# Output copy of the attention on VectorE, the last group's product behind the second tile's power, and the MLP's first low parts on VectorE alone

## The chip, the cores and the metric

The kernel runs on one core of a Trainium2 chip. The metric is the device time of one execution in microseconds. The engines are called by the profile's names: PE (TensorE, matmuls, with PEld for its weight loads), DVE (VectorE), ACT (ScalarE), POOL (GpSimd) and SP (SyncE, which here issues most DMAs). Each engine works through its own queue in order; semaphores tie the queues together.

## The reference

One layer for two groups of tokens, 256 context tokens and 2048 latent tokens, of width 1024. For each group, in float32:

```
h = RMSNorm(x) * (1 + scale1) + shift1
q, k, v, f = split(h @ w_in)                      # 4 heads x 2 halves x 64; v 4 x 128; f 4 x 128
a = softmax(q1 k1) - lam * softmax(q2 k2)         # differential attention, latent rows see 512 cached + 2048 keys
attn = RMSNorm(a @ v) * subln_g * (1 - lam_init)  # per head
four = real(fft2(f)) @ w_four
x += gate1 * (concat(attn, four) @ w_out)
h = RMSNorm(x) * (1 + scale2) + shift2
x += gate2 * (relu(h @ w1) ** 2 @ w2)             # 1024 -> 4096 -> 1024
```

The outputs are both groups' x and the context tokens' keys and values.

## The kernel before

**Products.** A float32 product is made of three fast products: each operand is split into a high part (a cast) and a low part (the value minus the high part), and `mm3` issues high x high (L95), high x low (L96) and low x high (L97). So ahead of every product there is a cast, mostly on ACT, and a subtraction, mostly on DVE.

**Stages.** Projection, Fourier mixing, attention (about 550 to 1244 us), output projection with the second norm (to 1460 us), the MLP's first product, the MLP's second product. Inside a stage the order of each engine's queue is the order in which the program calls its pieces (`tc.manual_schedule`).

**Attention.** Four heads, each in groups of 256 queries; a class `Group` holds a group's pieces as methods. A table of events (time, method) is filled for all groups and sorted by time, and that is the order in which the pieces are called; the time has no other meaning. Per group: scores on PE (`Ss`, L1081), row maxima on DVE (L1086), exps on ACT (`P0s`, `P1s`, L1105), the combination of the two softmaxes on POOL (L1120, L1121), transposes on PE (`pts`, L1136), high parts on ACT (`ahs`) and low parts on DVE (`als`, L1148), and the product with v into `po`. A group's end is `o1` to `o9`: `o1` copies the sum out of `po` to `oTs` (L1173), `o2` transposes it on PE (L1177), `o3` copies that to `os` (L1184), `o4` squares it on ACT (L1190), `o5` takes the power -1/2 on POOL, `o6` and `o7` send the result through memory and back as `rbs`, spread over all partitions, `o8` multiplies `oTs` by `rbs` on POOL (L1211), `o9` stores it as `att`. For the very last group everything from `o4` on is put in a list, LASTO, and called later, between pieces of the output projection.

**Output projection.** 18 tiles of 128 tokens, in the order `seq`. The first three are s0, s1, s2. `mix(i)` makes a tile's high part `mh` (L1603) and low part `ml` (L1605) on DVE; `w_split` splits w_out into `woh` (ACT, L1576) and `wol` (DVE, L1577 and L1580); `out_mm` issues the products, `out_post` applies the gate (L1623, L1624), `x_norm` makes the second norm. In the norm ACT sums squares (`nsqb`, L229), DVE scales (`nssb`, L230), POOL takes the power -1/2 (`nrsb`, L92), DVE multiplies (`xn`, L236); PE then transposes `xn` (`ptb`, L249).

**First product of the MLP.** A seven-product scheme (of Strassen's kind) over quarter matrices: ORDER = (1, 6, 2, 7, 5, 4, 3), one item of 12 PE products for each in a round, `pA` to `pD` being their sums. `h_parts` makes the high part `mhh` (ACT, L1502) and the low part `mhl` (DVE, L1506) of an activation operand of 128x1536; for the third to fifth operand the low part is split in two halves, POOL's and DVE's (L1511). `w_cast` makes a weight operand's `ophW` (ACT, L1468) and `oplW` (DVE, L1474). `mlp_ahead` loads, prepares and casts the first operands while the output projection still runs.

Of the kernel before, what the change touches and what calls it, by code (L numbers as in the profile page):

```python
# [21 lines left out]
KD = D // P  # L22
NP = 256
NS = 2048
NT = NP + NS
PAST = 512
H = 4
# [10 lines left out]
def f32(ap):  # L38
    return ap.bitcast(F32)


def body(tc, a, out):
    nc = tc.nc
    ctx = ExitStack()
    with ctx:
# [211 lines left out]
        right = ExitStack()  # L257
# [732 lines left out]
        with ExitStack() as c3_:  # L990
# [49 lines left out]
            class Group:  # L1040
# [130 lines left out]
                def o1(self):  # L1171
                    self.oT = self.op.tile([P, 256], F32, tag="oT", name=f"oT{self.nm}", bufs=1 if self.last else 3)
                    nc.scalar.copy(self.oT, self.po[:, 0:256])  # L1173

# [134 lines left out]
            for h in range(H):  # L1309
# [19 lines left out]
                for g in range(hd.ng):  # L1329
# [31 lines left out]
                    w = base + (AVS + 5) * T + 1.0 * u  # L1361
                    for t, fn in ((0, gr.o1), (0.4, gr.o2), (0.75 if gr.last else 4.25, gr.o3), (8.5, gr.o4), (9.2, gr.o5), (11.8, gr.o6), (16.3, gr.o7), (23.4, gr.o8), (26.0, gr.o9)):
                        if gr.last and t > 1:
                            LASTO.append(fn)
                        else:
                            add(w + t * u, fn)
# [122 lines left out]
        def h_parts(b, p):  # L1489
# [17 lines left out]

            def rest2():
                t = src[0][1]
                for V, c in ((nc.gpsimd, slice(2, 4)), (nc.vector, slice(0, 2))):  # L1510
                    V.tensor_sub(lo[:, c, :], t[:, c, :], f32(hi[:, c, :]))  # L1511

            if b == 0 and p in ORDER[2:5]:
                return high, rest2

            return high, rest
# [11 lines left out]
        def mlp_ahead(part):  # L1528

            if part == 0:  # L1530
                h_prep(0, ORDER[0])
            elif part == 3:
                for n in range(2):
                    if n:
                        h_prep(0, ORDER[n])
                    w_cast(n)
                    w_low()
                    if n == 0:
                        h_load(0, ORDER[3])
            elif part == 1:  # L1540
                h_load(0, ORDER[4])
                w_cast(2)
                w_cast(3)
            else:
                R = RAW[0]
                nc.vector.tensor_sub(R["a12"], R["a12"], R["s2"])
                R["s4"] = R["a12"]
# [6 lines left out]
        with c3o, ExitStack() as c4, ExitStack() as c4x, ExitStack() as c4w:  # L1554
# [44 lines left out]
            def mix(i):  # L1599
# [3 lines left out]
                nc.vector.tensor_copy(mh, mT)  # L1603
                for c in (slice(0, 2), slice(2, KD)) if i == s0 else (slice(0, KD),):
                    nc.vector.tensor_sub(ml[:, c, :], mT[:, c, :], f32(mh)[:, c, :])  # L1605
# [52 lines left out]
            with tc.manual_schedule():  # L1658
# [29 lines left out]
                x_norm(s0)  # L1688
                for fn in LASTO[3:]:
                    fn()  # L1690
                kv_even.close()
                ms1 = ctx.enter_context(tc.tile_pool(name="m_s1", bufs=2, side="right"))
                ms2s = ctx.enter_context(tc.tile_pool(name="m_s2s", bufs=2, side="right", reuse_waits="tile"))
                mix_load(seq[3])
# [3 lines left out]
                x_store(s1)  # L1698
                x_norm(s1)
                for n, i in enumerate(seq[2:], 2):  # L1700
                    if n == 2:
# [38 lines left out]
        with c5r, ExitStack() as c5:  # L1740
# [157 lines left out]
            with tc.manual_schedule():  # L1898
                for n, (q, p) in enumerate(ITEMS):
# [3 lines left out]
                    rest = None  # L1903
                    if n == 3:
                        mlp_ahead(2)
                        w_add(1, 0)
                    if n < 4:
# [6 lines left out]
                    if n == 5:  # L1914
                        high, rest = h_parts(0, 3)
                        high()
                    w_low()
                    for c in CASTS[n] if n < len(CASTS) else (n + LEAD + 1,):
# [247 lines left out]
```

## Time and profile before

| | |
|---|---|
| median of 3 runs (lowest to highest) | 2858.12 us (2855.85 to 2858.37) |
| profiled execution | 2859.23 us |
| its span | 2857.4 us |
| granted TensorE clock, mean | 0.996 |
| PE busy | 2826.0 us, 99% of the span |
| DVE busy | 1991.7 us, 70% |
| ACT busy | 1538.3 us, 54% |
| POOL busy | 1083.1 us, 38% |

The shares are means over stages that differ: in attention DVE, ACT and POOL are all busy most of the time, in the MLP's second product POOL hardly is. Rows of a timeline give start, duration, engine, line, operation, output <- input, and in brackets the idle time before and what ended it. Rows of the windows view give the stretch, its length, the busy time of PE, PEld, DVE, ACT and POOL with the number of instructions, the granted clock, the DMA share and GB/s. Records of matmuls overlap: the next one starts before the last one's end as shown.

### The profile page before, as it was taken

The page shows a single profiled execution, that of the slowest core. Times are in us where ns is not written, and L with a number is a line of the kernel's source. Part 1 is how long each engine was busy: PE and PEld are TensorE (multiplying, and loading weights), DVE is VectorE, ACT ScalarE, POOL GpSimd, SP SyncE. Part 2 cuts the span into 40 slices and gives each one's busy share as a digit, 9 for nine tenths or more (in the row PEclk, how much of TensorE's full clock was granted, in tenths as well). Part 3 has the DMA queues.
Part 4 walks back from the last instruction along what each step waited for, and adds up shares of the span by engine and source line. Part 5 has one row for each costly group of instructions (what it writes and reads, how often), then busy time and mean ns, then how long its engine had stood idle before and what let it go on. Part 6 is the DMA issues. An engine that isn't in the chain of part 4 may idle for free.

```text
span 2857.4 us, 43074 instructions
## 1 busy us (share of the span) xinstructions
PE 2826.0 (99%) x15029; PEld 2455.7 (86%) x15029; DVE 1991.7 (70%) x3357; ACT 1538.3 (54%) x3479; POOL 1083.1 (38%) x893
## 2 busy tenths in 40 slices
PE   8999999999999999999999999999999999999999
PEld 5888888688888888888889999999998888888887
DVE  7767887888888888864477777778775353445554
ACT  4333323798999989843356565566554332233221
POOL 1211223689999899942223333333332000000000
PEclk9999999999999999999999999999999999999999
DMA  7777767432222333156867667667647464445663
GB/s 285 220 209 200 232 208 240 163 108 55 80 75 53 112 63 85 40 137 207 251 209 232 224 240 234 218 224 239 227 167 256 147 202 138 136 144 186 206 205 111
DMA packets 404491, 497.69 MB, mean 174 GB/s; under 512 B 31427, under 2 KB 320304, under 8 KB 401202
## 3 DMA queue, kind: packets, MB, share of 16 engines
q1 hardware_dynamic: 398656, 484.09, 53.7%
q0 software_dynamic: 2064, 7.67, 0.8%
q10 hardware_dynamic: 3554, 3.17, 0.4%
q8 instruction: 119, 1.95, 0.3%
q14 instruction: 98, 0.80, 0.1%
HBM read 317.30 MB, written 179.62 MB: 174 GB/s over the span
## 4 chain that ended last, share of the span: by engine, by line
PE 54%; DMA 1%; DVE 0%; issue 0%; SPq 0%; POOL 0%; ACT 0%; DVEq 0%; POOLq 0%
PE ps L95 8%; PE ps L97 8%; PE ps L96 8%; PE pB L1782 2%; PE pB L1783 2%; PE pB L1781 2%; PE pC L1781 2%; PE pC L1782 2%; PE pC L1783 2%; PE pA L1781 2%; PE pA L1783 2%; PE pA L1782 2%; PE po L97 2%; PE po L95 2%; PE po L96 2%; PE pD L1783 1%
## 5 line engine op out<-in xcount | busy, mean ns | idle before, releaser
L1086 DVE TENSOR_REDUCE mxs<-Ss 128x1 f32<-128x512 f32 x636 | 405.8, 686 | 83.6 <-PE Ss L1081 73.3
L1443 DVE TENSOR_TENSOR sl<-sr,sh 128x768 fp32r<-128x768 f32 x168 | 161.8, 964 | 331.5 <-ACT sh L1442 331.1
L1121 POOL TENSOR_TENSOR P0s<-P0s,P1s 128x1024 f32<-128x1024 f32 (+2 forms) x128 | 377.2, 2946 | 10.7
L1442 ACT CAST sh<-sr 128x768 fp32r<-128x768 f32 x168 | 140.6, 838 | 418.3 <-PE ps L96 418.3
L1823 POOL TENSOR_TENSOR gs<-g,g 128x384 f32<-128x384 f32 x48 | 69.7, 1453 | 454.4 <-ACT g L1793 435.9
L1105 ACT ACTIVATE P1s<-Ss,mxs 128x512 f32<-128x512 f32 x318 | 215.4, 694 | 35.9 <-DVE mxs L1089 33.8
L95 PE MATMUL pj<-wh,hh 128*128 128x512 f32 x576 | 228.7, 397 | 2.0 <-DVE hh L556 2.0
L95 PE MATMUL ps<-thT,sh 128*128 128x512 f32 x585 | 227.6, 389 | 0.0
L96 PE MATMUL ps<-tlT,sh 128*128 128x512 f32 x585 | 227.6, 389 | 0.0
L97 PE MATMUL ps<-thT,sl 128*128 128x512 f32 x585 | 227.6, 389 | 0.0
L96 PE MATMUL pj<-wl,hh 128*128 128x512 f32 x576 | 227.0, 394 | 0.0
L97 PE MATMUL pj<-wh,hl 128*128 128x512 f32 x576 | 225.8, 392 | 0.0
L1105 ACT ACTIVATE P0s<-Ss,mxs 128x512 f32<-128x512 f32 x318 | 214.6, 692 | 4.9 <-DVE mxs L1089 4.0
L1136 PE MATMUL pts<-ident,P0s 128*128 128x128 f32 x1280 | 192.4, 274 | 4.5 <-DVE als L1148 1.8
L1081 PE MATMUL Ss<-KS0s,Qs 128*128 128x512 f32 x636 | 190.8, 421 | 0.4 <-ACT P1s L1105 0.4
L1081 PE MATMUL Ss<-KS1s,Qs 128*128 128x512 f32 x636 | 189.2, 422 | 1.5 <-ACT P0s L1105 1.1
L1792 ACT ACTIVATE g<-uz 128x384 f32<-128x384 f32 x144 | 75.7, 526 | 200.2 <-DVE uz L1815 170.6
L1136 PEld LDWEIGHTS pts<-ident,P0s 128*128 128x128 f32 x1280 | 152.3, 141 | 36.1 <-issue 5.2
L1120 POOL TENSOR_SCALAR P1s<-P1s,tots 128x1024 f32<-128x1024 f32 (+2 forms) x128 | 171.7, 1341 | 5.8
L1148 DVE TENSOR_TENSOR als<-pts,ahs 128x512 fp32r<-128x512 f32 x256 | 163.7, 681 | 8.6 <-ACT ahs L1143 8.6
L95 PE MATMUL ps<-ophT,sh 128*128 128x512 f32 x423 | 164.7, 389 | 1.1 <-DVE uz L1815 1.1
L96 PE MATMUL ps<-oplT,sh 128*128 128x512 f32 x423 | 164.6, 389 | 0.0
(539 smaller groups left out, 8030.8 us busy)
## 6 DMA issues: line engine op xcount, KB each, us to landing
sr<-sd SPq DMA_DIRECT2D x84, 768.0 KB, 4.5
a<-in_w SPq DMA_DIRECT2D x184, 256.0 KB, 4.2
sd<-gs SPq DMA_DIRECT2D x192, 192.0 KB, 1.9
sd<-g SPq DMA_DIRECT2D x144, 192.0 KB, 2.4
wm<-in_w_mod SPq DMA_DIRECT2D x32, 512.0 KB, 5.0
Qs<-qd SPq DMA_DIRECT2D x32, 512.0 KB, 5.4
b<-in_w SPq DMA_DIRECT2D x64, 256.0 KB, 5.5
b<-tsum SPq DMA_DIRECT2D x64, 256.0 KB, 4.6
```

What stands on the lines that cost most here:

```text
L95: nc.tensor.matmul(ps, lh, rh, start=first, stop=False)
L96: nc.tensor.matmul(ps, lh, rl, start=False, stop=False)
L97: nc.tensor.matmul(ps, ll, rh, start=False, stop=last)
L1081: nc.tensor.matmul(S[:, :w], self.Q[:, x, m, j * P:j * P + P], self.hd.KS[m][:, b * 512:b * 512 + w], start=(x == 0), stop=(x == 1))
L1086: nc.vector.tensor_reduce(self.mx[j][:, m, b:b + 1], self.S[j, m, b], axis=AX.X, op=ALU.max)
L1105: nc.scalar.activation(dst, S, AF.Exp, bias=self.mx[j][:, m, 6:7], accum_out=self.sm[j][:, m, b:b + 1])
L1120: nc.gpsimd.tensor_scalar(p, p, tot[:, 3:4], 0.0, op0=ALU.mult, op1=ALU.add)
L1121: nc.gpsimd.tensor_add(d, d, p)
L1136: nc.tensor.transpose(pt[:, c:c + P], self.p0[j][:, (kb + t) * P:(kb + t + 1) * P], ident)
L1781: nc.tensor.matmul(ps, wh[:, c], hh[:, k, :], start=first and k == 0, stop=False, skip_group_check=True)
L1782: nc.tensor.matmul(ps, wh[:, c], hl[:, k, :], start=False, stop=False, skip_group_check=True)
L1783: nc.tensor.matmul(ps, wl[:, c], hh[:, k, :], start=False, stop=k == 3, skip_group_check=True)
```

## The change

Five edits:

1. `o1` copies `po` to `oTs` on DVE, where it was on ACT (32 copies of 128x256).
2. `o3` of one group, the third from last of the last head, stands at 2.5 in the event table, where it was at 4.25.
3. `mix` splits the low part `ml` in 256 + 768 columns for the first two tiles; it did for the first.
4. The last group's `o8` and `o9`, its product on POOL and its store, and the pools that are closed and opened behind them, come behind the second tile's products, gate and norm; they were ahead of them.
5. In the MLP the low parts that were half POOL's are DVE's in one piece. Two calls move: `w_cast(2)` and `w_cast(3)` come behind the third operand's cast to its high part, and `mlp_ahead(2)` with `w_add(1, 0)` behind the sixth operand's.

```
@@ Group.o1
-                    nc.scalar.copy(self.oT, self.po[:, 0:256])
+                    nc.vector.tensor_copy(self.oT, self.po[:, 0:256])
@@ the event table
-                    ... (0.75 if gr.last else 4.25, gr.o3), ...
+                    ... (0.75 if gr.last else 2.5 if h == H - 1 and g == NS // 256 - 3 else 4.25, gr.o3), ...
@@ h_parts
-            def rest2():
-                t = src[0][1]
-                for V, c in ((nc.gpsimd, slice(2, 4)), (nc.vector, slice(0, 2))):
-                    V.tensor_sub(lo[:, c, :], t[:, c, :], f32(hi[:, c, :]))
-
-            if b == 0 and p in ORDER[2:5]:
-                return high, rest2
@@ mlp_ahead, part 1
-                w_cast(2)
-                w_cast(3)
@@ mix
-                for c in (slice(0, 2), slice(2, KD)) if i == s0 else (slice(0, KD),):
+                for c in (slice(0, 2), slice(2, KD)) if i in seq[:2] else (slice(0, KD),):
@@ the output projection
-                for fn in LASTO[3:]:
+                for fn in LASTO[3:4]:
                     fn()
-                kv_even.close()
-                ms1 = ...
-                ms2s = ...
                 mix_load(seq[3])
                 x_load(seq[3])
                 out_mm(s1, 0)
                 out_post(s1, 0)
                 x_store(s1)
                 x_norm(s1)
+                for fn in LASTO[4:]:
+                    fn()
+                kv_even.close()
+                ms1 = ...
+                ms2s = ...
@@ the MLP's items
                     rest = None
-                    if n == 3:
-                        mlp_ahead(2)
-                        w_add(1, 0)
                     if n < 4:
                         high, rest = h_parts(0, ORDER[n + 2])
                         high()
                         ...
+                    if n == 0:
+                        w_cast(2)
+                        w_cast(3)
+                    if n == 3:
+                        mlp_ahead(2)
+                        w_add(1, 0)
                     w_low()
```

Behind `mlp_ahead`, the lines of the changed kernel are ten lower than before (L1603 becomes L1593, L1577 becomes L1567). PE's and SP's queues keep their order. Three places of the other queues, in the order of instructions:

DVE in attention, around a group's output copy, as a difference (the numbers behind a name are those of head, group and buffer):

```order
 L1148 TENSOR_TENSOR als_1_0_5828<-pts_1_0_5765,ahs_1_0_5805 128x512
 L1148 TENSOR_TENSOR als_1_2_5832<-pts_1_2_5792,ahs_1_2_5810 128x512
+L1173 COPY oTs_0_5846<-po 128x256
 L1086 TENSOR_REDUCE mxs_3_0_5840<-Ss_3_0_0_0_5843 128x1
 L1086 TENSOR_REDUCE mxs_3_0_5840<-Ss_3_0_0_1_5853 128x1
```

The copy comes behind the low parts of the next group's first transposes and ahead of that round's first row maxima.

DVE at the passage from attention to the output projection, before:

```order
L1148 TENSOR_TENSOR als_7_16_14867<-pts_7_16_14837,ahs_7_16_14845 128x512
L1148 TENSOR_TENSOR als_7_18_14869<-pts_7_18_14847,ahs_7_18_14865 128x512
L1577 SCALAR_TENSOR_TENSOR wol_0_14952<-wout_13434,cols,woh_0_14944 128x512
L1603 CAST mh_14973<-wout_13436 128x1024
L1605 TENSOR_TENSOR ml_14974<-wout_13436,mh_14973 128x256
L1605 TENSOR_TENSOR ml_14974<-wout_13436,mh_14973 128x768
L1577 SCALAR_TENSOR_TENSOR wol_1_14953<-wout_13434,cols,woh_1_14945 128x512
```

and now:

```order
L1148 TENSOR_TENSOR als_7_16_14867<-pts_7_16_14837,ahs_7_16_14845 128x512
L1148 TENSOR_TENSOR als_7_18_14869<-pts_7_18_14847,ahs_7_18_14865 128x512
L1173 COPY oTs_7_14887<-po 128x256
L1567 SCALAR_TENSOR_TENSOR wol_0_14952<-wout_13434,cols,woh_0_14944 128x512
L1593 CAST mh_14973<-wout_13436 128x1024
L1595 TENSOR_TENSOR ml_14974<-wout_13436,mh_14973 128x256
L1595 TENSOR_TENSOR ml_14974<-wout_13436,mh_14973 128x768
L1567 SCALAR_TENSOR_TENSOR wol_1_14953<-wout_13434,cols,woh_1_14945 128x512
```

The last group's copy, which waits for the last product into `po`, stands ahead of the whole preparation of the output projection on DVE.

POOL behind the first output tiles, before (`nrsb` with the lower number is the first tile's power, the other the second's):

```order
L92 TENSOR_TENSOR nrsb_15118<-nssb_15115,mhalf 128x1
L1206 DMA rbs_7_15121<-rs_84 128x256
L1211 TENSOR_TENSOR oTs_7_14887<-oTs_7_14887,rbs_7_15121 128x256
L1215 DMA att_80<-oTs_7_14887 128x256
L92 TENSOR_TENSOR nrsb_15171<-nssb_15168,mhalf 128x1
```

and now:

```order
L92 TENSOR_TENSOR nrsb_15119<-nssb_15116,mhalf 128x1
L1206 DMA rbs_7_15122<-rs_84 128x256
L92 TENSOR_TENSOR nrsb_15163<-nssb_15160,mhalf 128x1
L1211 TENSOR_TENSOR oTs_7_14887<-oTs_7_14887,rbs_7_15122 128x256
L1215 DMA att_80<-oTs_7_14887 128x256
```

The second tile's power stands ahead of the last group's product, behind the issue of the DMA that this product waits for.

More of the change, by code (lines that the diff above doesn't have):

```diff
@@ L1361, in body @@
                     w = base + (AVS + 5) * T + 1.0 * u
-                    for t, fn in ((0, gr.o1), (0.4, gr.o2), (0.75 if gr.last else 4.25, gr.o3), (8.5, gr.o4), (9.2, gr.o5), (11.8, gr.o6), (16.3, gr.o7), (23.4, gr.o8), (26.0, gr.o9)):
+                    for t, fn in ((0, gr.o1), (0.4, gr.o2), (0.75 if gr.last else 2.5 if h == H - 1 and g == NS // 256 - 3 else 4.25, gr.o3), (8.5, gr.o4), (9.2, gr.o5), (11.8, gr.o6), (16.3, gr.o7), (23.4, gr.o8), (26.0, gr.o9)):
                         if gr.last and t > 1:
@@ L1688, in body @@
                 x_norm(s0)
-                for fn in LASTO[3:]:
+                for fn in LASTO[3:4]:
                     fn()
-                kv_even.close()
-                ms1 = ctx.enter_context(tc.tile_pool(name="m_s1", bufs=2, side="right"))
-                ms2s = ctx.enter_context(tc.tile_pool(name="m_s2s", bufs=2, side="right", reuse_waits="tile"))
                 mix_load(seq[3])
@@ L1699, in body @@
                 x_norm(s1)
+                for fn in LASTO[4:]:
+                    fn()
+                kv_even.close()
+                ms1 = ctx.enter_context(tc.tile_pool(name="m_s1", bufs=2, side="right"))
+                ms2s = ctx.enter_context(tc.tile_pool(name="m_s2s", bufs=2, side="right", reuse_waits="tile"))
                 for n, i in enumerate(seq[2:], 2):
```

## The prediction

> **What bounds the kernel now.** I read the shares of the engines first, then what ended TensorE's idle time line by line, then timelines and equal windows at the four places that the change touches.
>
> ```profile
> PE 2826.0 (99%) x15029; PEld 2455.7 (86%) x15029; DVE 1991.7 (70%) x3357; ACT 1538.3 (54%) x3479; POOL 1083.1 (38%) x893
> ```
>
> TensorE (PE) is busy for 2826.0 of 2857.4 us, so no edit gains unless it closes a gap of PE, and it loses wherever it opens one. Matmul records overlap, so I count a gap by the distance between starts: undisturbed, a 512-wide product starts 0.23 us after the last one and a 384-wide one 0.173.
>
> **The attention copy (o1 on VectorE).** Each steady group transposes its output after a copy `oTs` out of `po`. What held PE's weight loads for that transpose from 560 to 1240 us:
>
> ```profile
> L1177 PEld LDWEIGHTS po<-ident,oTs x62: 137/138/145, 574.0 to 1232.7; 128*128 128x128 f32 x62
> ...
>   ACT oTs L1173: 10.9, 27
> ```
>
> 27 waits, but the 10.9 us is no gain yet, since PE still has products running while the load waits. The gain comes from a usual group set beside one that doesn't wait (PE timelines: start, duration):
>
> ```profile
> 573.34 0.71 PE L1081 MATMUL Ss<-KS0s,Qs 128*128 128x512 f32 x2
> 574.04 0.44 PE L1177 MATMUL po<-ident,oTs 128*128 128x128 f32 x2
> 574.24 0.99 PE L1081 MATMUL Ss<-KS0s,Qs 128*128 128x512 f32 x3
> ...
> 1041.38 0.71 PE L1081 MATMUL Ss<-KS0s,Qs 128*128 128x512 f32 x2
> 1041.93 0.38 PE L1177 MATMUL po<-ident,oTs 128*128 128x128 f32 x2
> 1042.06 0.71 PE L1081 MATMUL Ss<-KS0s,Qs 128*128 128x512 f32 x2
> ```
>
> From the score products to the next ones it is 574.24 − 573.34 = 0.90 us in the usual group and 1042.06 − 1041.38 = 0.68 in the other: **0.22 us**. Why the copy is late, and who could do it sooner (ACT, then VectorE, DVE):
>
> ```profile
> 572.96 0.68 ACT L1105 ACTIVATE P1s<-Ss,mxs 128x512 f32<-128x512 f32 x1
> 573.62 0.37 ACT L1173 COPY oTs<-po 128x256 f32<-128x256 f32 x1
> ...
> 572.10 1.28 DVE L1148 TENSOR_TENSOR als<-pts,ahs 128x512 fp32r<-128x512 f32 x2
> 574.09 0.69 DVE L1086 TENSOR_REDUCE mxs<-Ss 128x1 f32<-128x512 f32 x1 [0.71 <-PE Ss L1081]
> ...
> L1184 DVE COPY os<-po x31: 412/415/424, 579.0 to 1235.4; 128x256 f32<-128x256 f32 x31
> ```
>
> ACT copies at 573.62, behind exps, and ends at 573.99. DVE is done at 573.38 and idle until 574.09. The copy's form is that of `os`, 0.415 us, so it ends near 573.8 and the reduction behind it does not move. The estimate: the load is ready where PE wants it. It cannot gain below 0 or above 0.22. The next bound is the loop through the other engines: in a stretch of four groups
>
> ```profile
> 685.37:773.40 88.03, 88.03 (x569) 75.03 (x570) 76.71 (x151) 80.18 (x227) 82.16 (x64) 1.00 0.27 55
> ```
>
> DVE is busy 76.7, ACT 80.2, GpSimd (POOL) 82.2 of 88.0 us; with 1.7 us more of copies DVE is still the least loaded. POOL leaves 5.9/4 = 1.5 us a group, seven times what a group shortens. So I take 0.22 for each of the 25 steady groups that wait outside the last stretch: **−5.6 us**.
>
> In the drain at the end of attention the two waits to be had are
>
> ```profile
> 1219.67 0.44 PE L1177 MATMUL po<-ident,oTs 128*128 128x128 f32 x2 [0.45 <-ACT oTs L1173]
> 1223.82 1.13 PE L1162 MATMUL po<-ahs,vf4s 128*128 128x256 f32 x4 [0.54 <-DVE os L1184]
> ...
> 1203.57:1233.50 29.93, 28.91 (x209) 25.86 (x208) 20.92 (x39) 22.75 (x63) 28.81 (x23) 1.00 0.17 30
> ```
>
> The second is what the moved `os` copy (o3 at 2.5) removes. But POOL is busy 28.81 of 29.93 us there and its last `P0s` is what the last transposes use, so PE meets POOL later instead: **0** (−1.0 if that cover is wrong).
>
> **The norm behind out projection (second tile).** POOL, DVE and windows (us, PE, PEld, DVE, ACT, POOL, granted clock):
>
> ```profile
> 1272.61 0.74 POOL L1211 TENSOR_TENSOR oTs<-oTs,rbs 128x256 f32<-128x256 f32 x1 [4.77 <-DMA rbs<-rs]
> 1274.26 0.58 POOL L92 TENSOR_TENSOR nrsb<-nssb,mhalf 128x1 f32<-128x1 f32 x1
> ...
> 1270.31 0.15 DVE L230 TENSOR_SCALAR nssb<-nssb 128x1 f32<-128x1 f32 x1 [1.27 <-ACT nsqb L229]
> 1274.87 0.75 DVE L236 TENSOR_SCALAR xn<-xo,nrsb 128x1024 f32<-128x1024 f32 x1 [4.40 <-POOL nrsb L92]
> ...
>   DVE xn L236: 2.3, 1
> ...
> 1273.68:1277.09 3.41, 1.32 (x10) 1.30 (x11) 2.19 (x3) 0.60 (x2) 1.13 (x2) 1.00 0.69 197
> 1277.09:1280.50 3.41, 3.41 (x9) 2.66 (x9) 2.77 (x3) 2.30 (x7) 2.25 (x2) 0.50 0.71 214
> ```
>
> The power's input is there at 1270.46, but the power starts at 1274.26, because POOL's queue holds the product `oTs`, which waits for a DMA, and its store ahead of it. Now it stands ahead: 1270.5 to 1271.1, so `xn` ends near 1271.9, before PE's queue comes to the transposes. That removes PE's 2.3 us wait, with the restart 2.5. In the window behind it the clock is 0.50 and nine products take 3.64 us instead of 9 × 0.231 = 2.08: 1.57 more. Together **−4.1**; −2.5 if the half clock has another cause. What is queued behind the power now is `oTs_7`'s product, which waits for its DMA as before (1272.61) and ends no later.
>
> [...]
>
> **The start of the MLP.** PE's three waits, the window behind them, and DVE and POOL meanwhile:
>
> ```profile
> 1466.31 0.44 PE L1783 MATMUL pA<-mhh,oplW 128*128 128x384 f32 x1 [1.13 <-DVE oplW L1474]
> 1469.12 0.41 PE L1781 MATMUL pB<-mhh,ophW 128*128 128x384 f32 x1 [0.81 <-DVE u L1805]
> 1471.05 0.44 PE L1782 MATMUL pB<-mhl,ophW 128*128 128x384 f32 x1 [1.51 <-DVE mhl L1511]
> ...
> 1471.65:1475.06 3.41, 3.41 (x13) 3.41 (x12) 3.41 (x5) 2.15 (x5) 0.00 (x0) 0.50 0.82 264
> ...
> 1463.92 4.58 DVE L1474 TENSOR_TENSOR oplW<-a,ophW 128x512 fp32r<-128x512 f32 x2
> ...
> 1463.09 4.86 POOL L1511 TENSOR_TENSOR mhl<-hr,mhh 128x768 fp32r<-128x768 f32 x2 [9.92 <-DMA hd<-hTb]
> ...
> L1506 DVE TENSOR_TENSOR mhl<-hr,mhh x14: 1746/1752/2052, 1453.9 to 1943.8; 128x1536 fp32r<-128x1536 f32 x14
> ...
> L1474 DVE TENSOR_TENSOR oplW<-a,ophW x140: 675/682/2331, 1456.9 to 2154.3; 128x512 fp32r<-128x512 f32 x140
> ```
>
> While POOL makes its two halves (4.86 us), DVE's two `oplW` take 4.58 instead of 2 × 0.68. With the whole low part on DVE, each costs 1.75 instead of DVE's half of about 0.96, three times +0.8, and the two `oplW` save 3.3. Laid one behind another by these durations in the new order, DVE ends the first low part at 1463.9, the `oplW` at 1464.5 and 1465.1, the next low part at 1467.2, the third at 1470.0 (its high part is cast only when its DMA has landed), the fourth at 1472.2. PE's four items of 12 products then wait 0.29, 0.73 and 0.14 us and end at 1464.67 + 4 × 2.08 + 1.16 = 1474.15, against 1478.78 before (the clock is not halved): −4.6. DVE itself, however, is only 2.5 ahead, since the two additions that stood ahead of the fourth low part now follow it, and it has no gap before 1489 us. PE would meet `oplW` and `u` of the next round and give back about 1.4. So **−3.2**, between −2.5 and −4.6.
>
> **The passage to the out projection, where I expect a loss.** DVE and ACT and PE there:
>
> ```profile
> 1241.36 1.24 DVE L1577 SCALAR_TENSOR_TENSOR wol<-wout,cols,woh 128x512 fp32r<-128x512 f32 x1
> 1242.51 0.68 DVE L1603 CAST mh<-wout 128x1024 fp32r<-128x1024 f32 x1
> 1243.23 1.29 DVE L1605 TENSOR_TENSOR ml<-wout,mh 128x256 fp32r<-128x256 f32 x2
> 1244.44 2.07 DVE L1577 SCALAR_TENSOR_TENSOR wol<-wout,cols,woh 128x512 fp32r<-128x512 f32 x3
> ...
> 1243.62 0.37 ACT L1173 COPY oTs<-po 128x256 f32<-128x256 f32 x1 [0.56 <-PE po L97]
> ...
> 1250.91 0.50 PE L97 MATMUL po<-woh,ml 128*128 128x512 f32 x1 [0.36 <-DVE ml L1605]
> ```
>
> On ACT the last group's copy stood behind nothing that PE wants next. On DVE it stands ahead of `wol_0`, `mh` and `ml`, and it waits until 1243.6 for PE's last product. What DVE did from 1241.36 to 1244.5 comes after 1244.0: `wol_0` to 1244.7, `mh` to 1245.3, `ml` in its two pieces to 1246.6, the other seven `wol` to 1251.0, the second tile's `mh` to 1251.6. The out projection's first product, ready at 1244.24 now, starts at 1245.35, and the second tile's low part, whose wait of 0.36 us the split 256 + 768 was to remove, is late again behind the whole row. PE passes 1251.25's place at 1252.61: **+1.4**. The bounds are 0 (DVE's queue catches up in PE's shadow) and +3.1 (two idles of about 1 us call forth a half clock, 1.7 as in the windows above).
>
> **The sum.** −5.6 + 0 − 4.1 − 3.2 + 1.4 = −11.5. The profiled execution took 2859.23 us, so 2847.7; the median of the runs shown, 2858.12, lies 1.1 below it, which gives **2846.6 us**, written 2847.
>
> **The rivals.**
> 1. The attention loop keeps its period. A group ends when exps, maxima and GpSimd's combination have gone round, and PE only moves its wait to the scores. For it speaks POOL's 82.2 of 88.0; against it the groups that already go without the wait. Then −5.9: 2852.3. Chance 0.14.
> 2. The passage halves the clock: +1.7, 2848.4. For it: the windows at 0.50 above, behind an idle of 2.3 us and behind three of 1.13, 0.81 and 1.51 close together; against it, both had more idle time than the 2 us spread here over 7. Chance 0.12. [...]
> 3. DVE sets the pace of the MLP's first rounds, so that the third term is −1: 2849. Chance 0.08.
> 4. **Slower.** The copy on DVE runs beside POOL as `oplW` does, 2.33 instead of 0.68 us, 3.4 times as long: 1.42 us. It would end at 574.8 instead of 573.99, PE would stand 0.73 us more in each of 25 groups, +18.3 instead of −5.6: 2846.6 + 23.9 = 2870.5. It decides from a copy of about 0.9 us on. Against it: 31 `os` copies, out of the same `po`, between 412 and 424 ns with POOL busy almost throughout. Chance 0.04. [...]
> 5. It does less than it says: the power is now early, but PE then waits for the out projection's sums, ACT's `nsqb`, for 2 us: 2850. Chance 0.05.
>
> **How the numbers follow.** The forecast keeps 0.57. This kernel's measurement can tell about 0.2% from no change, 5.7 us, so faster means below 2852.4. The forecast, rivals 2, 3 and 5 lie there whole and rival 1 about half; with something for a mishap in them that I do not see, faster 0.84, same 0.12, slower 0.04. The range goes from −15.5 (the drain's 1.0, the MLP's −4.6, the passage at 0 and half a microsecond more) to rival 1: 2842.5 to 2853.
>
> **What will show it.** Right: a row of `oTs` copies on DVE near 415 ns, the wait of L1177 for them under 2 us in sum, and a stretch of four groups shorter by 0.9 us; the `nrsb` before 1272 by the old time and no window at 0.50 after it; `oplW` never near 2.3 us before 1480; a wait of L95 for `mh` and of L96 or L97 for `wol` or `ml` at the passage. Wrong: an unchanged stretch with PE's wait moved to L1081 or L1136 (rival 1), a 0.50 window near 1248 (2), copies over 0.9 us (4).

## The result, and the profile after

| | before | changed |
|---|---|---|
| median of 14 runs (lowest to highest) | 2856.28 us (2854.71 to 2860.04) | 2850.23 us (2847.51 to 2853.88) |
| ratio to before, 95% interval | | 0.9977 [0.9969, 0.9986] |
| span of the profiled execution | 2857.4 us | 2851.9 us |

The change made the kernel faster by 0.23%, or 6 us, where 11.5 had been forecast. PE's instructions are the same in both kernels, so each stage can be read off as the difference of the starts of the same product in the two traces. The changed kernel's profiled execution, 2853.88 us, is the slowest of its 14, so the stages below are those of one execution and not of the median.

| product at (us) | before | changed | difference | in the stage | forecast |
|---|---|---|---|---|---|
| start of the attention | 540.17 | 541.07 | +0.90 | | |
| last scores of the attention | 1203.10 | 1199.90 | -3.20 | -4.10 | -5.6 |
| last output products | 1242.13 | 1238.93 | -3.20 | 0.00 | 0 |
| first output tiles | 1255.16 | 1254.92 | -0.24 | +2.96 | +1.4 |
| behind the second tile's norm | 1284.21 | 1279.83 | -4.39 | -4.15 | -4.1 |
| end of the output projection | 1455.25 | 1450.87 | -4.38 | 0.01 | 0 |
| second round of the MLP | 1478.78 | 1471.15 | -7.63 | -3.25 | -4.6 |
| third round of the MLP | 1500.07 | 1494.48 | -5.59 | +2.04 | +1.4 |
| near the end | 2850.19 | 2844.61 | -5.58 | 0.01 | 0 |

All numbers are in us; a minus means that the changed kernel is earlier. The +0.90 ahead of the attention lies where nothing was changed; it is the difference of two executions. The stages sum to -6.5.

**Attention.** What held PE's weight loads for the transpose, and the copy itself (lines of the changed kernel from 560 to 1240 us):

```profile
L1177 PEld LDWEIGHTS po<-ident,oTs x62: 137/140/143, 574.7 to 1228.5; 128*128 128x128 f32 x62
...
  DVE oTs L1173: 0.7, 2
...
L1173 DVE COPY oTs<-po x31: 411/414/425, 574.2 to 1228.0; 128x256 f32<-128x256 f32 x31
```

10.9 us in 27 waits have become 0.7 in 2, and the copy takes 414 ns. A usual group on PE's timeline:

```profile
707.42 0.71 PE L1081 MATMUL Ss<-KS0s,Qs 128*128 128x512 f32 x2
707.96 0.38 PE L1177 MATMUL po<-ident,oTs 128*128 128x128 f32 x2
708.10 0.48 PE L1081 MATMUL Ss<-KS0s,Qs 128*128 128x512 f32 x1
```

From scores to scores it is 708.10 - 707.42 = 0.68 us, where it was 0.90. But PE now waits for POOL at three places where it did not in the profiled execution of before. Around one of them, SP's issues, POOL and PE:

```profile
967.94 0.42 SPq L1029 DMA_DIRECT2D Vs<-vd  x1
...
970.94 0.33 SPq L1206 DMA_DIRECT2D rbs<-rs  x1
...
982.22 0.75 POOL L1211 TENSOR_TENSOR oTs<-oTs,rbs 128x256 f32<-128x256 f32 x1 [5.15 <-DMA rbs<-rs]
...
987.43 0.55 PE L1136 MATMUL pts<-ident,P0s 128*128 128x128 f32 x3 [0.32 <-POOL P0s L1121]
...
1010.13 0.55 PE L1136 MATMUL pts<-ident,P0s 128*128 128x128 f32 x3 [0.48 <-POOL P0s L1121]
```

The same product on POOL in before:

```profile
982.98 0.75 POOL L1211 TENSOR_TENSOR oTs<-oTs,rbs 128x256 f32<-128x256 f32 x1 [3.78 <-DMA rbs<-rs]
```

POOL stands idle for 5.15 us, waiting for `rbs`, which was issued 3.0 us behind the next head's values `Vs` (2560 KB). Its first DMA packet starts at 978.86, 0.2 us behind the start of the last one of `Vs` (978.65), and its last one ends at 981.57, 10.6 us after the issue. What POOL then combines comes too late for PE twice (0.32 and 0.48 us; the third place is in the drain, shown with e7).

**Passage to the output projection.** PE, DVE and the window:

```profile
1240.90 0.44 PE L1177 MATMUL po<-ident,oTs 128*128 128x128 f32 x2 [0.52 <-DVE oTs L1173]
1242.26 0.47 PE L95 MATMUL po<-woh,mh 128*128 128x512 f32 x1 [0.92 <-ACT osqs L1190]
...
1244.16 0.80 PE L96 MATMUL po<-wol,mh 128*128 128x512 f32 x1 [0.73 <-DVE wol L1567]
1244.75 0.63 PE L97 MATMUL po<-woh,ml 128*128 128x512 f32 x1
...
1240.42 0.43 DVE L1173 COPY oTs<-po 128x256 f32<-128x256 f32 x1 [2.19 <-PE po L97]
...
1244.00:1247.40 3.40, 3.24 (x8) 2.57 (x9) 3.40 (x7) 3.40 (x7) 1.14 (x2) 0.51 1.13 125
```

DVE stood idle 2.19 us for the copy, PE then waits twice for what DVE prepares, and the next window has the clock at 0.51. The profile puts the first of these waits down to ACT's `osqs`, but in before the same product started 0.2 us behind the transpose, ahead of any `osqs`. Here DVE's `mh` ended at 1242.11, 0.15 us ahead of the product, and that is what it waited for.

**Norm of the second tile.** POOL, DVE and the window:

```profile
1270.30 0.57 POOL L92 TENSOR_TENSOR nrsb<-nssb,mhalf 128x1 f32<-128x1 f32 x1 [2.72 <-DVE nssb L230]
...
1270.91 0.75 DVE L236 TENSOR_SCALAR xn<-xo,nrsb 128x1024 f32<-128x1024 f32 x1 [0.70 <-POOL nrsb L92]
...
1273.60:1277.00 3.40, 3.40 (x19) 2.88 (x18) 1.79 (x3) 2.91 (x8) 1.82 (x3) 1.00 0.85 242
```

The power starts 0.1 us behind its input, PE has no gap in this window and the clock is 1.00.

**Start of the MLP.** PE's waits, ACT's casts of the fifth and sixth operand, and two `oplW` on DVE:

```profile
1463.06 0.44 PE L1774 MATMUL pB<-mhl,ophW 128*128 128x384 f32 x1 [0.37 <-DVE mhl L1506]
1465.97 0.45 PE L1774 MATMUL pC<-mhl,ophW 128*128 128x384 f32 x1 [0.56 <-DVE mhl L1506]
1469.14 0.44 PE L1774 MATMUL pD<-mhl,ophW 128*128 128x384 f32 x1 [0.82 <-DVE mhl L1506]
1472.14 0.45 PE L1775 MATMUL pA<-mhh,oplW 128*128 128x384 f32 x1 [0.47 <-DVE oplW L1474]
...
1480.87 0.44 PE L1773 MATMUL pB<-mhh,ophW 128*128 128x384 f32 x1 [0.30 <-DVE u L1797]
1489.78 0.44 PE L1855 MATMUL ptf<-ident,xnf 128*128 128x128 f32 x2 [0.31 <-DVE xnf L1846]
...
1462.64 1.48 ACT L1502 CAST mhh<-hr 128x1536 fp32r<-128x1536 f32 x1 [1.46 <-DMA hr<-hd]
1465.82 1.48 ACT L1502 CAST mhh<-hr 128x1536 fp32r<-128x1536 f32 x1 [1.18 <-DMA hr<-hd]
...
1459.59 1.29 DVE L1474 TENSOR_TENSOR oplW<-a,ophW 128x512 fp32r<-128x512 f32 x2
```

The two `oplW` take 1.29 us instead of 4.58, and there is no half clock: it is 1.00 from 1457.2 to 1474.2 us. But two casts wait for the loads of their operands, and the low parts behind them come late.

### The profile page after: what moved, and what is told of

The parts are those of the page before. It is cut to its first block, busy times and chain, and to the rows that moved or that the text cites. A ratio compares the mean times of both kernels' runs of the same rounds, so it can differ in the third digit from the quotient of the medians.

```text
span 2851.9 us, 43035 instructions
## 1 busy us (share of the span) xinstructions
PE 2819.3 (99%) x15029; PEld 2458.8 (86%) x15029; DVE 1998.7 (70%) x3390; ACT 1530.2 (54%) x3447; POOL 1078.0 (38%) x890
## 4 chain that ended last, share of the span: by engine, by line
PE 91%; DMA 3%; DVE 2%; ACT 2%; issue 1%; POOL 1%; SPq 0%; ACTq 0%; DVEq 0%; POOLq 0%
PE Ss L1081 10%; PE ps L95 8%; PE ps L97 8%; PE ps L96 8%; PE pts L1136 5%; PE po L96 4%; PE po L97 4%; PE po L95 4%; PE pj L97 4%; PE pj L96 4%; PE pj L95 4%; PE pB L1773 2%; PE pC L1774 2%; PE pC L1775 2%; PE pB L1774 2%; PE pC L1773 2%
## 5 line engine op out<-in xcount | busy, mean ns | idle before, releaser
L1143 ACT CAST ahs<-pts 128x512 fp32r<-128x512 f32 x256 | 147.1, 608 | 33.9 <-PE pts L1136 32.5
```

The costliest lines, as they stand in the source:

```text
L1143: (nc.vector.tensor_copy if self.drain and kb == FULL[0] else nc.scalar.copy)(t, self.pt[kb])
```

## The experiments

All kernels of one table row ran beside the kernel before on the same chip; ratios are to that. The stage columns are differences of the starts of the same products, against the profiled execution of before shown above, as in the first table. They tell what the times, with intervals of 0.08 to 0.15% to either side, cannot, but each is one execution. Theory 1 and theory 2 are those of the expectations, written before each run.

| run | median, us | ratio [95%] | 540-556 | 556-1203 | 1242-1255 | 1268-1455 | 1455-1500 |
|---|---|---|---|---|---|---|---|
| the changed kernel | 2850.23 | 0.9977 [0.9969, 0.9986] | 0.0 | -4.1 | +3.0 | -4.1 | -1.2 |
| the same again, another chip (f1) | 2853.15 | 0.9969 [0.9957, 0.9980] | -2.4 | -0.9 | +1.4 | -4.2 | -1.1 |
| e1, last copy on ACT | 2852.10 | 0.9967 [0.9954, 0.9980] | -2.4 | -1.2 | -0.5 | -3.2 | -1.2 |
| e2, all copies on ACT | 2853.76 | 0.9972 [0.9962, 0.9982] | -2.4 | +2.5 | -0.8 | -3.9 | -1.4 |
| e3, fourth edit alone | 2855.86 | 0.9979 [0.9970, 0.9988] | -1.5 | +1.6 | -0.1 | -4.1 | +0.1 |
| e4, fifth edit alone | 2858.91 | 0.9994 [0.9985, 1.0003] | -2.4 | +0.6 | 0.0 | +1.6 | -1.4 |
| e5, values loaded later | 2848.76 | 0.9959 [0.9945, 0.9973] | -2.4 | -5.6 | +4.4 | -4.2 | -1.3 |
| e6, stores later | 2854.33 | 0.9973 [0.9962, 0.9984] | -2.4 | -2.0 | +1.4 | -4.2 | -0.5 |
| e7, without the second edit | 2852.61 | 0.9969 [0.9959, 0.9980] | -2.4 | -1.6 | +1.5 | -4.2 | -1.2 |
| e8, e1 + e5 + e6 | 2849.21 | 0.9957 [0.9942, 0.9972] | -2.4 | -5.5 | -0.4 | -3.8 | -0.6 |
| f3, e1 + e5 | 2846.51 | 0.9948 [0.9934, 0.9962] | -2.4 | -5.9 | -0.6 | -4.2 | -1.3 |
| f2, f3 + stores last | 2845.89 | 0.9944 [0.9931, 0.9957] | -2.4 | -5.8 | -0.4 | -4.2 | -1.5 |
| g1, f2 + sixth load ahead | 2846.94 | 0.9948 [0.9934, 0.9961] | -2.4 | -5.6 | -0.4 | -4.1 | -0.9 |

The column 540-556 is the first thing to read. It lies ahead of every edit, and yet it takes one of three values, 0, -1.5 or -2.4: in the profiled executions of before and of the changed kernel, PE's clock was halved in two windows there (0.50 from 543.22 and 550.05 us, and from 544.31 and 551.14), in that of e3 in one, in the others in none. Over the whole execution the mean clock was 0.996 in before, 0.998 in the changed kernel, in e3 and in e5 (whose windows lie at the passage), and 0.999 in the others. The same stretch of before and of e7:

```profile
540.00:543.20 3.20, 1.67 (x6) 0.87 (x7) 2.79 (x7) 3.20 (x11) 3.12 (x3) 1.00 0.01 3
543.20:546.60 3.40, 3.40 (x12) 2.71 (x12) 1.52 (x3) 3.40 (x11) 3.32 (x2) 0.50 0.00 0
...
550.00:553.40 3.40, 3.40 (x12) 2.71 (x11) 1.76 (x4) 3.07 (x9) 3.32 (x2) 0.51 0.19 74
```

```profile
540.00:543.20 3.20, 1.67 (x6) 0.59 (x4) 2.94 (x6) 3.20 (x11) 3.12 (x2) 1.00 0.01 3
543.20:546.60 3.40, 2.91 (x16) 2.16 (x16) 2.11 (x5) 3.40 (x12) 3.32 (x3) 1.00 0.00 0
...
550.00:553.40 3.40, 3.40 (x21) 2.49 (x20) 2.84 (x5) 3.08 (x10) 3.32 (x3) 1.00 0.05 18
```

The idle time of PE is the same (1.67 us busy of 3.20), the clock behind it is not. It is worth 2.4 us, and what is won there is lost again in the next column, in part or whole, unless POOL's wait is mended (e5): f1, with the same instructions as the changed kernel, has -2.4 and -0.9 where that has 0.0 and -4.1. The two columns are therefore best read together.

**e1: the last group's copy on ACT.**

```
-                    nc.vector.tensor_copy(self.oT, self.po[:, 0:256])
+                    (nc.scalar.copy if self.last else nc.vector.tensor_copy)(self.oT, self.po[:, 0:256])
```

> The changed kernel, with the copy of the very last group alone back on ScalarE. Theory 1: the passage to the output projection costs the changed kernel 3.0 us, 1.4 because the copy stands ahead of the whole preparation on VectorE and 1.6 because two idles of TensorE of about 1 us call forth a half clock; both go, TensorE is 3.0 us earlier from the second output tile on than in the changed kernel, no product of the first output tile stands 0.427 us behind the last one, about 2847.3 us. Theory 2: the half clock there has another cause than this copy; only 1.4 us go, the spacing of 0.427 us stays, about 2848.8 us.

PE at the passage in e1:

```profile
1241.95 0.44 PE L1177 MATMUL po<-ident,oTs 128*128 128x128 f32 x2 [0.46 <-ACT oTs L1173]
1242.15 0.47 PE L95 MATMUL po<-woh,mh 128*128 128x512 f32 x1
```

The first product follows the transpose at once, the stage goes from +2.96 to -0.54, and no product is spaced 0.427 us: the starts from 1242.15 to 1244.59 us lie 0.23 to 0.31 apart. That is theory 1. At 3.5 us it is 0.5 more than expected, and the split of the second tile's `ml` accounts for it: the six profiled runs with that split and the last copy on ACT stand at -0.4 to -0.8 there, e3 and e4, without the split, at -0.1 and 0.0. The time tells no more: 0.9967, against 0.9977 and 0.9969 for the changed kernel on two chips. The columns of f1, e6 and e7 show where theory 1 was too simple: with the copy on DVE and no half clock the passage costs 1.4 to 1.5 us, with one window 3.0 (after), with two 4.4 (e5). So the half clock there is not a fixed price. f1 has the same three idles as the changed kernel, 0.52, 0.92 and 0.73 us, and no half clock. In the nine profiled runs with the last copy on ACT, before among them, there is none either. The norm's stage is only -3.2 in e1, since PE waits there for ACT's `hTb`; why is left open.

**e2: the copy on ACT in every group.**

```
-                    nc.vector.tensor_copy(self.oT, self.po[:, 0:256])
+                    nc.scalar.copy(self.oT, self.po[:, 0:256])
```

> The changed kernel with the copy on ScalarE in every group, the other four edits as they are. Theory 1: the copy is worth 0.22 us in each usual group, of which GpSimd takes back 1.5 us beside the prompt groups, so that TensorE ends the attention 4.1 us later than in the changed kernel, and the passage is 3.0 us shorter: about +1.1 us, 2851.3 us. Theory 2: the groups shorten for another reason (the other edits do not touch the attention before its last groups, so this has little for it): TensorE ends the attention as in the changed kernel, -3.0 us, 2847.2 us.

The waits for the transpose are back as in before (from 560 to 1240 us):

```profile
L1177 PEld LDWEIGHTS po<-ident,oTs x62: 137/141/145, 572.9 to 1233.3; 128*128 128x128 f32 x62
...
  ACT oTs L1173: 11.0, 27
```

From 540 to 1203 us e2 stands +0.1 to before, the changed kernel -4.1, f1 -3.3, e1 -3.6, e6 -4.4, e7 -4.0: so the attention shortens by the copy, as theory 1 has it, and not without it. Its size is less sure than expected: e3 and e4, with the copy on ACT too, stand at +0.1 and -1.8. By the means of these runs (-3.9 with the copy on DVE, -0.4 on ACT, before included) the copy is worth 3.5 us with the load as it stands, not 5.6.

Away from the waits for POOL the size is as read from two groups. Between 1035 and 1200 us of before, where six groups waited for the copy, the ten profiled runs with it on DVE gain 1.2 to 1.5 us on before, and e2, e3 and e4, with it on ACT, 0.0 to 0.1. What spreads the totals is the wait for `rbs`, and that wait does not need the shorter groups. In e2, with the copy on ACT, POOL stands as follows at the place shown above:

```profile
985.13 0.75 POOL L1211 TENSOR_TENSOR oTs<-oTs,rbs 128x256 f32<-128x256 f32 x1 [5.79 <-DMA rbs<-rs]
```

In the eight profiled runs besides before that have the load as it stands, this wait is 4.9 to 5.8 us, and PE waits for POOL behind it in all of them, e2 (1.54 and 0.31 us), e3 (0.73 and 0.33) and e4 (0.29) included. The profiled execution of before, with 3.78 us and no such wait of PE, is the lowest of the nine. So the stage of before that everything here is compared with is a favourable one.

**e3 and e4: one edit alone, on the kernel before.**

e3 takes the fourth edit, e4 the fifth, as in the diff of the change.

> The kernel before with the fourth edit alone, the last group's product and store behind the second tile's power. Theory 1: the wait for the power and the half clock behind it are one thing: -4.1 us between the second tile's transposes and the fourth tile's products, no window at 0.50 there, 2852.2 us. Theory 2: the half clock comes from something else in that stretch: -2.5 us, with the window at 0.50 still there, 2853.8 us.

> The kernel before with the fifth edit alone, the MLP's low parts on VectorE and the casts moved. Theory 1: the start of the MLP is now set by the loads of the activation operands, issued as soon as a buffer comes free and 5 to 6 us under way with the DMA engines full: TensorE gains 4.5 us up to the fifth item and gives back 3.3 in the next three rounds, -1.2 us in all, 2855.1 us. Theory 2, the prediction's: VectorE sets the pace and the loads do not count: -3.2 us, 2853.1 us.

In e3 the stage between 1268 and 1284 us is -4.15, with no half clock: theory 1 to the tenth. The time, 0.9979 [0.9970, 0.9988], is some 6 us less than before's; the stages of its profile sum to -4.1. e4, which keeps the wait, shows that its price is not fixed:

```profile
1276.40 1.94 PE L249 MATMUL ptb<-ident,xn 128*128 128x128 f32 x8 [3.91 <-DVE xn L236]
```

PE waited 3.91 us instead of 2.3, since the DMA that POOL's product waited for came later (the product started at 1273.26, in before at 1272.61), and the stage is 1.5 us longer than in before. In the MLP e4 gains 4.6 us up to 1473 and gives back 3.2 by 1500: -1.4, near theory 1 (-1.2) and far from the prediction's -3.2. The time, 0.9994 [0.9985, 1.0003], doesn't tell the two apart.

**e5: the values' load behind the norm factors'.**

```
-                add(base - 14 * T + 0.7 if h else 0.9 * T, hd.load_v)
+                add(base - 14 * T + 3.2 if h else 0.9 * T, hd.load_v)
```

> The changed kernel, with the load of the next head's values issued behind the load of one group's norm factors instead of ahead of it; nothing else. In the changed kernel GpSimd stands 3.3 to 5.1 us at 628, 804 and 982 us, its product of a group's output waiting for the 128 KB of norm factors that were issued 1.6 us behind 2560 KB of values. Theory 1: this wait is why GpSimd is late at the prompt groups and why the shorter groups gave 4.1 us of the 5.6 forecast. Then the three waits fall to under 1.5 us, TensorE no longer waits for GpSimd at the prompt groups (0.59 and 0.77 us near 987 and 1009 us), and from 556 to 1203 us the gain on the kernel before is 5.4 us or more where it is 4.1 now: about -1.5 us on the changed kernel. Theory 2: GpSimd's own work in the prompt groups, some 5 us more than in a usual group, sets it: its waits for the load go but TensorE's stay, 0 us.

What POOL's products waited for from 560 to 1203 us, in the changed kernel and in e5:

```profile
L1211 POOL TENSOR_TENSOR oTs<-oTs,rbs x28: 728/744/762, 603.7 to 1198.5; 128x256 f32<-128x256 f32 x28
...
  DMA rbs<-rs: 12.3, 3
```

```profile
L1211 POOL TENSOR_TENSOR oTs<-oTs,rbs x28: 733/742/770, 602.8 to 1195.5; 128x256 f32<-128x256 f32 x28
...
  DMA rbs<-rs: 1.8, 2
```

12.3 us became 1.8, PE no longer waits for POOL at the groups of the context tokens (the prompt groups of the expectation), and the stage from 556 to 1203 us is -5.59 (f3, f2, g1 and e8: -5.5 to -5.9), on top of the -2.4 ahead of it. That is theory 1, and 25 groups at 0.22 us are 5.5. At 982 us of the changed kernel `rbs` needed 10.6 us from its issue to its last packet; in e5 it needs 5.4 there. The kernel before with this edit alone was not run, so how much the edit would give without the shorter groups is open; by the waits of e2 and e3 above it would give something. In e5 the passage costs 4.4, with two windows at half clock:

```profile
1240.60:1244.00 3.40, 2.78 (x7) 2.21 (x8) 3.40 (x6) 3.40 (x7) 0.00 (x0) 0.50 1.41 193
1244.00:1247.40 3.40, 3.40 (x10) 2.63 (x9) 3.30 (x6) 1.73 (x4) 2.24 (x3) 0.50 0.54 111
```

**e6: the last tile's stores behind the sixth operand's load.**

```
-                    x_store(i)
+                    if i != LAST:
+                        x_store(i)
...
                             h_load(0, ORDER[n + 5])
+                            x_store(LAST)
```

> The changed kernel, with the two stores of the last output tile (256 KB each) issued behind the load of the MLP's sixth operand instead of ahead of it. Theory 1: the loads of the activation operands set the start of the MLP by their bytes on full DMA engines; with 512 KB less ahead of it the fifth operand's load lands about 1.4 us earlier, the sixth's, which then shares with the stores, at least 0.7 earlier; TensorE's waits of 0.72 and 0.98 us for the fifth and the sixth low part shrink by 0.7 each at least, and -0.5 to -1.4 us remain behind 1500 us. Theory 2: not bytes but the moment when a buffer comes free sets the sixth load (its issue at 1459.69 and the 6.1 us under way are as with the stores ahead), so that only the fifth operand's wait shrinks and nothing remains behind 1500 us: 0 us.

Neither theory holds. The fifth operand's wait goes, as both expected, but the sixth's grows:

```profile
1463.70 1.47 ACT L1502 CAST mhh<-hr 128x1536 fp32r<-128x1536 f32 x1 [2.58 <-DMA hr<-hd]
...
1467.03 0.45 PE L1775 MATMUL pD<-mhl,ophW 128*128 128x384 f32 x1 [1.35 <-DVE mhl L1506]
```

ACT stands 2.58 us for it instead of 1.18, and the stage falls from -1.2 to -0.5. The load was issued at 1456.91 and used at 1463.70, 6.8 us instead of 6.1: the stores, issued at 1457.29 and 1457.77, have landed only at 1465.04, so they are still under way beside it.

**e7: without the second edit.**

```
-(0.75 if gr.last else 2.5 if h == H - 1 and g == NS // 256 - 3 else 4.25, gr.o3)
+(0.75 if gr.last else 4.25, gr.o3)
```

> The changed kernel without the second edit (one group's output copy for the norm back at its old place). Theory 1: what that edit saves before 1224 us is waited for again at GpSimd's last combination (1.08 us at 1229): TensorE waits 0.5 us more for the copy at 1220 us, 0.5 less at 1229, and is at the same place by 1236 us, 0.0 us. Theory 2: the edit is worth its wait: +0.5 us at 1242.

In e7 the wait for `os` is back (first row). In the changed kernel PE waits for POOL 10 us later instead (second row):

```profile
1220.05 1.13 PE L1162 MATMUL po<-ahs,vf4s 128*128 128x256 f32 x4 [0.55 <-DVE os L1184]
```

```profile
1230.28 0.55 PE L1136 MATMUL pts<-ident,P0s 128*128 128x128 f32 x3 [0.81 <-POOL P0s L1121]
```

At 1224 us the changed kernel has gained 1.1 in the drain, e7 0.3; at 1242 both have 0.0. That is theory 1: the edit is worth nothing as long as POOL is late behind it.

**e8, f1, f3 and f2: what the parts come to together.** e8 is the changed kernel with the edits of e1, e5 and e6, f3 with those of e1 and e5. f2 is f3 with the stores at the seventh item of the MLP:

```
+                    if n == 6:
+                        x_store(LAST)
```

> The changed kernel with the last group's copy on ScalarE, the values' load behind the norm factors' and the last tile's stores behind the sixth operand's load, all three together. By theory 1 of each: -3.0 at the passage to the output projection (-3.5 in the run that had this alone), -1.5 in the attention, -0.5 to -1.4 in the MLP's start, so about 5 us less than the changed kernel and some 0.35 to 0.45% less than the kernel before. If the terms eat one another, as GpSimd ate the earlier start of the attention, it is no more than 3 us.

> The changed kernel as it is, to have it on the same chip as the two below. Theory 1: between 1243 and 1255 us it loses 1.5 us to the queue order on VectorE in every run and 1.5 more for each window of 3.4 us at half clock, whose place depends on the run (none in two of the profiled runs of this order, one in one, two in one); behind 1500 us it stands 5 to 8 us ahead of the profiled run before, the spread being windows at half clock at the attention's start and here.

> The changed kernel with the last group's copy on ScalarE and the values' load behind the norm factors'. By the runs of each alone: from 556 to 1203 us 1.5 us less than the changed kernel, at the passage 1.9 to 3.5 less, nothing else; 3 to 5 us less than the changed kernel.

> The one above, with the last tile's two stores issued behind the loads of the next weights, so that they share the DMA engines with neither the fifth nor the sixth operand's load. Theory 1: the sixth operand's load is what TensorE waits for at the MLP's start, and it is as long under way as there are bytes beside it: TensorE's waits for the fifth and sixth low part (0.72 and 0.98 us in the changed kernel, 0 and 1.79 with the stores beside the sixth load) come to under 0.8 together, and from 1455 to 1500 us the gain on the kernel before is 1.5 to 2.2 us where it is 1.2 in the changed kernel. Theory 2: VectorE's queue and the last tile's norm set the rounds behind it whatever the loads do: the waits shrink but by 1500 us the gain is the same 1.2.

e8's stages add up as those of its parts did alone; its time, 2849.21 us from four runs, is 3.9 us below that of f1 on the same chip, between the two cases expected. f1, f3 and f2 ran side by side: the changed kernel (f1) is 9.1 us below before there, where it was 6 on the first chip, and the two intervals overlap. f3 takes 6.6 us less than f1, more than the 3 to 5 expected, f2 7.3. Against before f2 is at 0.9944 [0.9931, 0.9957], the changed kernel at 0.9969 [0.9957, 0.9980]. f2's MLP stage is -1.48, at the edge of theory 1's range and not -1.2, but its waits are not where theory 1 had them:

```profile
1461.39 0.45 PE L1775 MATMUL pD<-mhl,ophW 128*128 128x384 f32 x1 [1.18 <-DVE mhl L1506]
...
1458.07 1.48 ACT L1502 CAST mhh<-hr 128x1536 fp32r<-128x1536 f32 x1 [1.80 <-DMA hr<-hd]
```

By distance of starts PE's two waits are 0.08 and 1.35 us, 1.43 together where under 0.8 was expected. The sixth load still takes 5.9 us from its issue at 1452.21. 512 KB less beside it saved it only 0.3.

**g1: the sixth operand loaded without waiting for a buffer.** f2, with

```
+        def h_direct(b, p):
+            hi = hp[p].tile(..., name=f"mhh{b}_{p}")
+            lo = hp[p].tile(..., name=f"mhl{b}_{p}")
+            nc.sync.dma_start(f32(lo), hop[p][b])
+            DIR[b, p] = (lambda: nc.scalar.copy(hi, f32(lo))), (lambda: nc.vector.tensor_sub(lo, f32(lo), f32(hi)))
...
-                            h_load(0, ORDER[n + 5])
+                            h_direct(0, ORDER[n + 5])
```

> The kernel with the late stores, and the sixth operand of the MLP loaded straight into the tile of its low part (high part cast from there, low part subtracted in place), so that its load does not wait for the buffer of the third operand. Theory 1: with the stores away the sixth load still took 5.9 us from its issue, so what is late is the issue, 2.5 us behind the fifth's because a buffer must come free; issued ahead of the fifth's, it is there in time, the fifth comes a little later, TensorE's two waits go from 1.43 us together to under 1.0, and from 1455 to 1500 us the gain on the kernel before goes from 1.5 to 1.8 us or more. Theory 2: both loads together are bound by the DMA engines, which were full (share 1.0) then: whichever comes second is as late as the sixth is now, the waits stay at 1.4 us or more, and the gain stays 1.5 or falls.

ACT's casts, PE and the windows:

```profile
1453.14 1.48 ACT L1502 CAST mhh<-hr 128x1536 fp32r<-128x1536 f32 x1 [2.31 <-DMA hd<-hTb]
...
1457.04 1.48 ACT L1517 CAST mhh<-mhl 128x1536 fp32r<-128x1536 f32 x1
...
1456.46 0.44 PE L1784 MATMUL pB<-mhl,ophW 128*128 128x384 f32 x1 [1.35 <-DVE mhl L1506]
...
1449.90:1453.20 3.30, 3.30 (x20) 3.30 (x20) 2.99 (x4) 0.99 (x4) 0.00 (x0) 1.00 1.02 355
1453.20:1456.50 3.30, 1.34 (x7) 0.76 (x6) 1.85 (x2) 3.30 (x3) 0.00 (x0) 1.00 1.00 392
```

The sixth operand is there in time, the fifth too, and now the cast of the fourth is late by 2.31 us: its high part is written where `hTb` lay, and the store of `hTb`, issued at 1448.08 just behind the sixth load, ended only at 1453. The stage falls to -0.9. Theory 1 falls, and theory 2 holds in its result (no less waiting with the DMA engines full, a share of 1.02 and 1.00 at 355 and 392 GB/s), though it was a store and not a load that came second. In e6, f2 and g1 alike, a new order of these transfers only chose what is late. That the bytes in all set the start of the MLP fits them, but f2, where 512 KB less saved the sixth load 0.3 us, does not bear it out, and it stays open what the 5.9 us of that load are made of. A version with fewer bytes there, or with the loads a whole tile earlier, wasn't tried.

## Why the prediction was right or wrong

The forecast was faster, and it was faster, by half of what was said: -6 us for -11.5 (-9 on f1's chip). The time lies in the predicted range, near its upper end. How near the total comes is in part luck, since it moves by 0.9 to 1.6 us with every half-clock window that an execution has or has not. Two sums are off by little: 25 groups at 0.22 us are 5.5 and not 5.6, and the lower end of the range adds up to -15.8 and not -15.5.

1. **The norm: right.** -4.1 forecast, -4.15 measured, in both halves: the wait and the half clock went together, in every profiled run with the edit (12), and both before and e4, without it, have the half clock (0.50 from 1277.09 us in before; in e4 the eight transposes behind the wait took 1.94 us, in before, ahead of its window, 1.07).
2. **The attention: the mechanism right, its cover wrong.** 0.22 us a group came as read from two groups, and 25 of them as soon as e5 let them through. The step "POOL leaves 5.9/4 = 1.5 us a group, seven times what a group shortens" failed. That slack is the mean of four usual groups from 685 to 773 us, where POOL waits for no load. At 628, 804 and 982 us it stands 3.3 to 5.1 us waiting for a small DMA behind 2560 KB, and there it has nothing to spare for shorter groups. The load came forward with the groups at 982 us: `Vs` was issued 2.1 us earlier than in before, and POOL was ready 2.1 us earlier, but `rbs` was complete only 0.95 us earlier (last packet at 981.57 for 982.52). Why POOL's wait there is longer in the eight other profiled runs with this load than in that of before stays open. The term was mis-sized by 1.5 to 2 us: -4.1 in the profiled pair, 3.5 by the means over the runs, for 5.6.
3. **The drain: right.** 0 forecast, 0.00 measured, and e7 shows the cover that was named: 0.8 us gained and taken back by POOL's last combination.
4. **The passage: the order right, the clock not.** The queue costs 1.4 to 1.5 us, as forecast from DVE's rows. The half clock, a rival with a chance of 0.12, came in two of five profiled runs with this order, once with one window (the changed kernel) and once with two (e5): +3.0 and +4.4. It should have been a part of the term, not a rival. The idles ahead of it in the changed kernel were of 0.5, 0.9 and 0.7 us.
5. **The MLP: wrong in size, by 2.** The step that the operands would be cast in time, with waits of 0.29, 0.73 and 0.14 us, failed. Only the fifth load was taken into account; the sixth, issued when the third operand's buffer came free, came 5.9 to 6.1 us after its issue, with the DMA engines full (a share of 0.99 from 1460.6 to 1467.4 us of the changed kernel). By distances of starts PE's waits for the low parts were 0.53, 0.72 and 0.98, and the gain at the second round is 3.25 instead of 4.6. What VectorE takes back behind it was forecast at 1.4 and is 2.04: `oplW`, `u` and the last tile's norm, each about half a microsecond.
6. **The rivals.** That the attention keeps its period fell: the groups shortened. That the copy is slowed by POOL fell with 411 to 425 ns for all copies. That DVE sets the MLP's first rounds gave the right size (-1), but of the 2 us that were missing 1.35 came from the late operands and only 0.64 from what DVE takes back. That PE would wait 2 us for the sums behind the early power fell with the whole -4.15.

## What to carry to other kernels

Before slack of an engine in a stage covers a gain, look at what its idle time waits for, and whether that moves too. Here POOL was ready 2.1 us earlier at 982 us and the DMA it waited for only 0.95 us earlier, and the small transfer was as late as the large one issued ahead of it on the same queue: the first packet of `rbs` (128 KB) started 0.2 us behind the last one of `Vs` (2560 KB). When a copy goes to the engine that also prepares the next stage, the last copy of the loop is a case of its own, since it puts a wait for the old stage ahead of the whole new one (here 2.19 us of idle time on DVE, and 1.4 to 1.5 us of PE's time). And a profile is one draw where idle time meets the clock (the same stretch had two half-clock windows, one or none here): compare stage by stage over the same instructions, and look for half-clock windows first, also where nothing was changed.

## What the runs showed of the hardware

The half clock behind the same idle time is there in some executions and not in others: at the attention's start in two windows (before, after), in one (e3) or in none (the eleven others), at the passage in one, two or none. A window was 3.4 us long in the traces of before and of the changed kernel. At the attention's start two cost PE 2.4 us and e3's one 0.9; at the passage one cost 1.6 (+3.0 beside +1.4) and two 3.0 (+4.4).

In the stretches read here, how much PE was idle just ahead does not tell the cases apart. With PE busy for 1.67 of 3.20 us, the stretch behind had the clock at 0.50 in before and at 1.00 in e7; with 1.56 of 3.40 us from 546.60 on it had 0.51 in before, and with 1.55 it had 1.00 in e7. At the passage the changed kernel, with idles of 0.52, 0.92 and 0.73 us, had 1.61 us busy in the 3.40 us from 1240.60 on and then the half clock; f1, with the same three idles, had none. What decides between the two is left open.
